# Row sums of softmax weights: a product with a column of ones in place of transposes and a reduction

## The chip, the cores and the metric

The kernel runs on one core of one Trainium2 chip. Five engines work side by side, each through its own queue in order: TensorE (PE; its weight loads are listed as PEld), VectorE (DVE), ScalarE (ACT), GpSimd (POOL), and SyncE (SP), which issues all DMAs here. Matmul results land in PSUM (eight banks of 128 partitions by 512 float32), all else is in SBUF or in device memory. The metric is the device time of one execution in microseconds (us).

## What is computed

One layer of a streaming encoder, float32, 2048 rows of width 1024. The input is projected once (`u = x @ w_in`), and its columns feed three groups: forgetting attention (6 heads of 64, causal), an mLSTM (4 heads of 96) and cross-attention into 256 memory tokens (4 heads of 64). Each group's output is gated, all are concatenated, projected by `w_out`, added to `alpha * x` and normalised. The change touches the softmax of the two attentions:

```python
logits = einsum('bhqd,bhkd->bhqk', q_blk, kh) + c_blk[..., :, None] - c[..., None, :]
p = softmax(where(causal, logits, -inf), axis=-1)     # forgetting attention
out = einsum('bhqk,bhkd->bhqd', p, vh)
...
p = softmax(einsum('bhsd,bhmd->bhsm', qh, kh), axis=-1)   # memory attention
out = einsum('bhsm,bhmd->bhsd', p, vh)
y = concatenate([y_fox * silu(fz), y_ml * silu(mz), y_mem * silu(rz)]) @ w_out
return layer_norm(alpha * x + y)
```

## The kernel before

**Order.** The kernel is written as many small generators (threads). A planner (`Machine`, L135 to L268) runs them once, ahead of time: each thread yields the next instruction or the next buffer that it wants, the planner keeps a clock for every engine, adds an estimated cost to each instruction (`Op.cost`, L91 to L113), and always issues what can start first, ties going to a fixed priority (`PRIO`). The order in which it issues is the order of each engine's queue on the chip. So a changed cost or a removed instruction can shift the order on all engines. All instructions are issued from one line, L214, so the profile's groups are told apart by their tiles.

**Precision.** Large products run in a reduced float32 format in three passes on split operands (`h` and `l`: a high part and the rest). Plain float32 matmuls stand only in the mLSTM, on four heads of 96.

**Stages.** The first 1040 us or so are projections (tiles `pj<-h,h`, `pj<-l,h`, `pj<-h,l`) with the attention between them: each (head, block of 512 queries) is an item, 24 of the forgetting and 16 of the memory attention. Then follow the mLSTM units and the output tiles (`pj<-h,yh` and so on) with their layer norm.

**An item.** `att_max` computes scores of queries by keys (`mx<-km,qm`) for row maxima, which go through a small transpose (`mx<-ident_r,r`) and a DMA into an extra row of the query tile. `att_qk` computes the scores again with keys on partitions and queries along columns (`st<-qm,km`, `st<-qb,kb`, four chunks of 128 keys per block). `att_exp` makes from each chunk the weights twice on ACT (`ph` rounded, `p` exact) and the low part `pl` on DVE; `acc`, the sum over chunks of `p`, is kept by POOL. It has 128 partitions by 512 queries, and what is still missing of a softmax denominator is the sum over its 128 partitions. `att_pv` multiplies by the values into a bank `o`.

**The end of an item** (`att_end`, L702) takes `o` to SBUF and then forms the denominators. Four transposes on PE turn the four 128x128 pieces of `acc` into a bank `mx` (`mx<-ident_r,acc`), and one DVE reduction along columns leaves 128x4 sums in `den` (`den<-mx`). Two heads share a `den` of 128x8. When both are there, `pair_end` (L729) takes the reciprocal, splits it in two parts (`r`), transposes them (`mx<-ident_r,r`, 16x128), moves them by four small DMAs into `rb`, spreads them over partitions by a matmul with `sel`, and scales `y`. Then the gate and the store into `yt_scr` follow. The PSUM tag `mx` has two banks, which `att_max`, `att_end` and `pair_end` share.

Of the kernel before, what the change touches and what calls it, by code (L numbers as in the profile page):

```python
# [12 lines left out]
F32 = mybir.dt.float32  # L13
# [3 lines left out]
ALU = mybir.AluOpType  # L17
AX = mybir.AxisListType
# [3 lines left out]
P = 128  # L22
# [51 lines left out]
class Op:  # L74


    def __init__(self, eng, fn, args, kw):
        self.eng, self.fn, self.args, self.kw = eng, fn, args, kw
        ap = [a for a in args if hasattr(a, "tensor")]
        out = kw.get("out", ap[0] if ap else None)  # L80
        ins = ap[1:] if "out" not in kw else ap
        ins = ins + [v for k, v in kw.items() if k != "out" and hasattr(v, "tensor")]
        self.out = out.tensor.name
        self.ins = [a.tensor.name for a in ins]
        size = lambda a: math.prod(a.shape[1:])
        cols = size(out)
        wide = max([cols] + [size(a) for a in ins])

        there = [a for a in ins if a.tensor.space == "SB" and size(a) > 1]
        self.port = len(there) > 1 if eng in ("DVE", "POOL") else False  # L90
        if eng == "PE":  # L91
            f32 = ins[0].dtype == F32
            if f32 and fn.__name__ != "transpose":
                self.cost = 2.0 * max(2.0 * cols / 2.4, 112.0)
            else:
                self.cost = max((2.0 if f32 else 1.0) * cols / 2.4 + 14.0, 110.0)
        elif eng == "ACT":
            self.cost = 70.0 + 0.835 * wide + 115.0 * sum(hasattr(kw.get(a), "tensor") for a in ("bias", "scale"))
        elif fn.__name__ == "tensor_tensor_scan":
            self.cost = 60.0 + 2.3 * wide  # L100
        elif eng == "DVE":
            one = fn.__name__ in ("tensor_scalar", "tensor_copy")
            columns = sum(size(a) == 1 for a in ins)
            self.cost = 69.0 + (0.521 if one else 1.042) * wide + 60.0 * columns
        elif eng == "POOL":
            if kw.get("op") == ALU.pow:
                self.cost = 290.0 + 170.0 * cols
            else:
                self.cost = 120.0 + (2.15 if fn.__name__ == "tensor_tensor" else 0.95) * wide
        else:  # L110
            self.cost = 475.0
            self.nbytes = 4 * math.prod(out.shape)
            self.far = 800.0 if kw["in_"].tensor.space == "DRAM" else 0.0  # L113
# [21 lines left out]
class Machine:  # L135
# [22 lines left out]
    def free(self, *tiles):  # L158
        for t in tiles:
            nm = t.tensor.name  # L160
            tag, obj = self.tag_of.pop(nm)
            self.seq += 1
            time = max(self.wr.get(nm, (0.0, ""))[0], self.rd.get(nm, 0.0))
            heapq.heappush(self.slots[tag], (time, self.seq, obj))
# [51 lines left out]
    def spawn(self, gen, prio):  # L216
        self.seq += 1
        self.step(Thread(gen, prio, self.seq), None)
# [99 lines left out]
def kernel(ctx: ExitStack, tc: tile.TileContext, xt, x, wg, memt, wm, wo, cw, gb, ng, lg, lb, out):  # L318
# [20 lines left out]
    for tag_, n_ in BUFS.items():  # L339
        m.tag(tag_, n_)  # L340
    PE, ACT, DVE, POOL, SP = (Engine(a, b) for a, b in (("PE", nc.tensor), ("ACT", nc.scalar), ("DVE", nc.vector),
                                                         ("POOL", nc.gpsimd), ("SP", nc.sync)))
    mm = PE.matmul
    now = m.issue

    def const(shape, dt, name):
        return cp.tile(shape, dt, tag=name, name=name)
# [4 lines left out]
    def dma(out, in_):  # L352
        fix = lambda a: a.bitcast(F32) if a.dtype == F32R else a
        return SP.dma_start(out=fix(out), in_=fix(in_))
# [11 lines left out]
    ident = ident_r.bitcast(F32)  # L366
# [9 lines left out]
                           base=0, channel_multiplier=-1))  # L376
    ones_c = const([FH, 1], F32, "ones_c")
    now(POOL.memset(ones_c, 1.0))
    mhalf = const([P, LH], F32, "mhalf")
    now(POOL.memset(mhalf, -0.5))  # L380
    gb_sb = const([P, 14], F32, "gb_sb")
# [295 lines left out]
    def att_pv(it):  # L677

        yield lambda: turn["pv"] == it["i"]
        o = yield Alloc("o")  # L680
        held, nch = None, len(it["chunks"])
        for ci, (km, kb, j, i, q0, dg) in enumerate(it["chunks"]):
            nq = BLK - q0
            last = ci == nch - 1
            yield lambda: ci in it["w"]
            ph, pl = it["w"].pop(ci)
            v_ = it["v"](i, j)
            yield mm(o[:, q0:BLK], v_, ph[:, 0:nq], start=(ci == 0), stop=False)
            free(ph)
            if it["hold"] and ci == 0:  # L690
                held = (v_, pl)
            else:
                yield mm(o[:, q0:BLK], v_, pl[:, 0:nq], start=False, stop=last and not it["hold"])
                free(pl)
            if last and it["hold"]:
                yield mm(o, *held, start=False, stop=True)
                free(held[1])
        turn["pv"] += 1
        it["pv_done"]()
        spawn(att_end(it, o), PRIO["fin"])  # L700

    def att_end(it, o):  # L702


        hh, key = it["hh"], it["ykey"]
        hs, other = slice(64 * hh, 64 * hh + 64), slice(64 - 64 * hh, 128 - 64 * hh)
        if hh == 0:
            ybox[key] = yield [Alloc("y", [P, BLK]), Alloc("sm", [P, 8], F32, "den")]
        yield lambda: key in ybox
        y, den = ybox[key]  # L710
        yield ACT.copy(y[hs, :], o[other, :])
        yield DVE.tensor_tensor(y[hs, :], o[hs, :], y[hs, :], op=ALU.add)
        free(o)
        yield lambda: it["added"] == len(it["chunks"]) - 1
        acc = it["acc"]
        t_ = yield Alloc("mx")
        for s in range(4):
            yield PE.transpose(t_[:, s * P:(s + 1) * P], acc[:, s * P:(s + 1) * P], ident)
        free(acc)
        yield DVE.tensor_reduce(den[:, 4 * hh:4 * hh + 4], t_.rearrange("p (s k) -> p s k", s=4), axis=AX.X,  # L720
                                op=ALU.add)
        free(t_)
        yleft[key] = yleft.get(key, 2) - 1
        if not yleft[key]:
            spawn(pair_end(it, y, den), PRIO["fin"])
# [3 lines left out]
    def pair_end(it, y, den):  # L729


        r_ = yield Alloc("sm", [P, 2, 2, 4], F32R, "r16")
        d2 = den.rearrange("p (h s) -> p h s", h=2)
        yield [DVE.reciprocal(den, den),
               DVE.tensor_copy(r_[:, :, 0, :], d2),
               DVE.tensor_tensor(r_[:, :, 1, :], d2, r_[:, :, 0, :].bitcast(F32), op=ALU.subtract)]
        free(den)
        t_ = yield Alloc("mx")
        yield PE.transpose(t_.bitcast(F32R)[0:16, 0:P], r_.rearrange("p a b c -> p (a b c)"), ident_r)
        free(r_)  # L740
        rr = yield Alloc("rr", [16, P], F32R)
        yield DVE.tensor_copy(rr, t_[0:16, 0:P])
        free(t_)
        rb = yield Alloc("rb")
        for h in range(2):
            for i in range(2):
                yield dma(out=rb[32 * h + i:32 * h + i + 1, :], in_=rr[8 * h + 4 * i:8 * h + 4 * i + 4, :])
        free(rr)
        t_ = yield Alloc("mx")
        yield mm(t_, sel[0:66, :], rb[0:66, :], start=True, stop=True)  # L750
        free(rb)
        yield DVE.scalar_tensor_tensor(y, y, 0.5, t_, op0=ALU.mult, op1=ALU.mult)
        free(t_)
        yield lambda: it["zk"] in zbox
        z_ = zbox.pop(it["zk"])
        b, k = it["dst"]
        yield POOL.tensor_tensor(y, y, z_, op=ALU.mult)
        free(z_)
        h_, l_ = yield [Alloc(YTAGS, [P, BLK], F32R, "yh"), Alloc(YTAGS, [P, BLK], F32R, "yl")]
        yield ACT.copy(h_, y)  # L760
        yield POOL.tensor_tensor(l_, y, h_.bitcast(F32), op=ALU.subtract)
        free(y)
        for i, t_ in enumerate((h_, l_)):
            yield dma(out=yt_scr[b][i][:, k, :], in_=t_)
            free(t_)
        yparts[b] += 1
        if sum(yparts) == 5 * NBLK:
            late.extend(("acc", "ph", "pl", "y", "qb", "p"))
# [109 lines left out]
    cols = {}  # L878
# [583 lines left out]
```

## Time and profile before

| | before |
|---|---|
| Time, median of 3 runs (lowest to highest) | 1351.32 us (1348.97 to 1353.2) |
| Time of the profiled execution | 1350.54 us |
| Its span | 1348.8 us |
| Mean granted clock of TensorE | 0.989 |
| Transposes `mx<-ident_r,acc` on PE | 160, from 84.6 to 1121.3 us |
| Reductions `den<-mx` on DVE | 40, from 87.5 to 1122.4 us |

The profile is one execution. Groups are printed as line, engine, operation, out<-in with tile names (a number behind a name is left out), partitions and shapes, count, then busy us, mean ns of one, and the engine's idle time just before them with what ended it. Timeline rows are start (us), duration (us), engine, operation, tiles and count; a bracket at the end holds the idle time before the row and who ended it. The duration of a PE row contains its way through the array, and the next one starts before it ends, so PE's pace is read from starts.

### The profile page before, as it was taken

How to read it: one execution, taken by the hardware profiler on the slowest of the kernel's cores; microseconds unless marked ns; L12 is line 12 of the kernel's file. 1: busy time of each engine (PE TensorE's matmuls, PEld its weight loads, DVE VectorE, ACT ScalarE, POOL GpSimd, SP SyncE). 2: the span in 40 equal slices, each digit the busy share in tenths (PEclk: the TensorE clock that was granted, in tenths of full speed). 3: DMA queues.
4: the chain of work that ended last, by engine and by line, in shares of the span. 5: the costliest groups of instructions: out<-in, count | busy, mean ns of one | idle time of the engine just before them, and what ended most of it. 6: DMA issues, size and time to landing. Idle time of an engine off the chain costs nothing. (4 is left out here: it accounts for less than half of the span.)

```text
span 1348.8 us, 20536 instructions
## 1 busy us (share of the span) xinstructions
PE 1303.4 (97%) x6648; PEld 1102.1 (82%) x6648; DVE 1011.3 (75%) x2042; ACT 639.6 (47%) x1347; POOL 483.3 (36%) x430
## 2 busy tenths in 40 slices
PE   7999999999999999999999999999999889899997
PEld 7889987877888878988878978887778567788886
DVE  6694457888886578668777787879889788576764
ACT  6343254645654454423545546354463666455400
POOL 3002021334351101310644737263461676455210
PEclk9999999999999999999999999999999799999999
DMA  7624356742336672271421341335227648999761
GB/s 273 200 63 137 125 162 218 242 146 88 122 132 228 229 220 78 96 227 64 138 54 38 109 128 38 106 122 169 87 77 252 194 127 234 274 246 286 227 210 48
DMA packets 176731, 209.50 MB, mean 155 GB/s; under 512 B 15936, under 2 KB 113488, under 8 KB 176624
## 3 DMA queue, kind: packets, MB, share of 16 engines
q1 hardware_dynamic: 176624, 208.19, 49.2%
q8 instruction: 53, 0.87, 0.3%
q14 instruction: 54, 0.44, 0.1%
HBM read 124.88 MB, written 74.41 MB: 148 GB/s over the span
## 5 line engine op out<-in xcount | busy, mean ns | idle before, releaser
L214 POOL TENSOR_TENSOR acc<-acc,p 128x512 f32<-128x512 f32 (+2 forms) x232 | 315.6, 1360 | 434.8 <-ACT p L214 189.3
L214 PE MATMUL pj<-h,h 128*128 128x512 f32 (+3 forms) x1144 | 425.4, 372 | 11.7 <-ACT h L214 9.8
L214 PE MATMUL pj<-l,h 128*128 128x512 f32 (+3 forms) x1144 | 419.3, 367 | 0.6 <-DVE l L214 0.4
L214 PE MATMUL pj<-h,l 128*128 128x512 f32 (+3 forms) x1144 | 418.4, 366 | 0.0
L214 PEld LDWEIGHTS pj<-h,h 128*128 128x128 f32 x1144 | 217.0, 190 | 41.0 <-ACT h L214 11.2
L214 PEld LDWEIGHTS pj<-l,h 128*128 128x128 f32 x1144 | 216.9, 190 | 28.7 <-DVE l L214 2.7
L214 PEld LDWEIGHTS pj<-h,l 128*128 128x128 f32 x1144 | 215.9, 189 | 25.5 <-DVE l L214 0.6
L214 DVE TENSOR_TENSOR pl<-p,ph 128x512 fp32r<-128x512 f32 (+2 forms) x191 | 183.9, 965 | 34.1 <-ACT p L214 29.4
L214 ACT ACTIVATE ph<-st 128x512 fp32r<-128x512 f32 (+2 forms) x224 | 122.8, 555 | 99.4 <-PE st L214 89.5
L214 DVE TENSOR_TENSOR l<-raw,h 128x512 fp32r<-128x512 f32 (+2 forms) x170 | 111.9, 678 | 40.1 <-ACT h L214 38.5
L214 ACT ACTIVATE p<-st 128x512 f32<-128x512 f32 (+2 forms) x232 | 125.5, 546 | 32.2 <-POOL acc L214 16.8
L214 ACT CAST h<-raw 128x512 fp32r<-128x512 f32 (+2 forms) x170 | 96.3, 580 | 70.9 <-DMA raw<-in_wg_dram 48.5
L214 DVE TENSOR_REDUCE mp<-mx 128x1 f32<-128x512 f32 x144 | 95.9, 683 | 22.6 <-PE mx L214 21.8
L214 PE MATMUL st<-qm,km 68*128 68x512 f32 (+2 forms) x272 | 104.5, 384 | 7.7 <-ACT p L214 4.5
L214 PE MATMUL st<-qb,kb 128*128 128x512 f32 (+2 forms) x272 | 110.1, 405 | 0.0
L214 PE MATMUL pj<-h,yh 128*128 128x512 f32 (+1 forms) x264 | 106.9, 405 | 3.2 <-DVE yl L214 2.2
L214 PE MATMUL o<-pl,v 128*128 128x512 f32 (+2 forms) x272 | 104.1, 387 | 6.2 <-DVE pl L214 5.8
L214 PE MATMUL pj<-l,yh 128*128 128x512 f32 (+1 forms) x264 | 102.2, 387 | 0.0
L214 PE MATMUL pj<-h,ylo 128*128 128x512 f32 (+1 forms) x264 | 102.0, 386 | 0.0
L214 PE MATMUL mx<-km,qm 66*128 66x512 f32 (+2 forms) x304 | 97.0, 357 | 2.8 <-issue 1.2
L214 PE MATMUL o<-ph,v 128*128 128x512 f32 (+2 forms) x224 | 84.7, 379 | 0.0
L214 POOL TENSOR_TENSOR y<-y,zs 128x512 f32<-128x512 f32 x20 | 29.5, 1477 | 140.0 <-DVE y L214 80.3
(183 smaller groups left out, 1902.4 us busy)
## 6 DMA issues: line engine op xcount, KB each, us to landing
raw<-in_wg_dram SPq DMA_DIRECT2D x52, 256.0 KB
raw<-in_wg_dram SPq DMA_DIRECT2D x48, 192.0 KB
v<-v_all SPq DMA_DIRECT2D x36, 256.0 KB
raw<-in_xt_dram SPq DMA_DIRECT2D x32, 256.0 KB
yh<-yt_scr SPq DMA_DIRECT2D x32, 256.0 KB
ylo<-yt_scr SPq DMA_DIRECT2D x32, 256.0 KB
xr<-in_x_dram SPq DMA_DIRECT2D x32, 256.0 KB
out_dram<-xr SPq DMA_DIRECT2D x32, 256.0 KB
```

Of the source, the lines that this page charges most:

```text
L214: op.fn(*op.args, **op.kw)
```

## The change

A constant tile `ones_p`, 128x1, is filled with ones. In `att_end` the four transposes of `acc` become four matmuls with the piece of `acc` as weights and `ones_p` as the moving side: each gives a 128x1 column, the sum over partitions, so that four columns of an `mx` bank hold what the reduction gave. The reduction on DVE goes; in its place stands the reciprocal of these 128x4 sums, straight from PSUM into `den`, and the reciprocal of 128x8 in `pair_end` goes. The planner's cost of a plain float32 matmul is lowered for one column, from 2 x 112 to 2 x 64 ns.

```diff
             if f32 and fn.__name__ != "transpose":
-                self.cost = 2.0 * max(2.0 * cols / 2.4, 112.0)
+                self.cost = 2.0 * max(2.0 * cols / 2.4, 112.0 if cols > 1 else 64.0)
...
+    ones_p = const([P, 1], F32, "ones_p")
+    now(POOL.memset(ones_p, 1.0))
...
         for s in range(4):
-            yield PE.transpose(t_[:, s * P:(s + 1) * P], acc[:, s * P:(s + 1) * P], ident)
+            yield mm(t_[:, s:s + 1], acc[:, s * P:(s + 1) * P], ones_p, start=True, stop=True)
         free(acc)
-        yield DVE.tensor_reduce(den[:, 4 * hh:4 * hh + 4], t_.rearrange("p (s k) -> p s k", s=4), axis=AX.X,
-                                op=ALU.add)
+        yield DVE.reciprocal(den[:, 4 * hh:4 * hh + 4], t_[:, 0:4])
...
-        yield [DVE.reciprocal(den, den),
-               DVE.tensor_copy(r_[:, :, 0, :], d2),
+        yield [DVE.tensor_copy(r_[:, :, 0, :], d2),
```

On PE, in the projections of the second half of the sequence, the burst of the first item there keeps its place. Before:

```order
L214 MATMUL pj_7586<-l_5511,h_6980 128x512
L214 MATMUL pj_7586<-h_5510,l_6981 128x512
L214 MATMUL mx_7619<-ident_r,acc_7297 128x128 x4
L214 MATMUL pj_7586<-h_5513,h_6980 128x512
L214 MATMUL pj_7586<-l_5514,h_6980 128x512
L214 MATMUL pj_7586<-h_5513,l_6981 128x512
```

The same place on PE with the change:

```order
L214 MATMUL pj_7574<-l_5503,h_6968 128x512
L214 MATMUL pj_7574<-h_5502,l_6969 128x512
L214 MATMUL mx_7607<-ones_p,acc_7285 128x1 x4
L214 MATMUL pj_7574<-h_5505,h_6968 128x512
L214 MATMUL pj_7574<-l_5506,h_6968 128x512
L214 MATMUL pj_7574<-h_5505,l_6969 128x512
```

Only the four instructions differ; their neighbours are the same matmuls (names are numbered anew). On DVE, the last pair of the first half, before:

```order
L214 TENSOR_REDUCE den_6579<-mx_6592 128x4
L214 TENSOR_TENSOR pl_6604<-p_6600,ph_6599 128x512
L214 TENSOR_TENSOR g_1387_6104<-pj_6555,gb_sb 128x14
L214 TENSOR_TENSOR pl_6609<-acc_6598,ph_6539 128x512
L214 TENSOR_TENSOR vs_6621<-pj_6555,vs_6621 128x6x64
L214 TENSOR_TENSOR y_6578<-o_6593,y_6578 64x512
L214 TENSOR_REDUCE den_6579<-mx_6649 128x4
L214 RECIPROCAL den_6579<-den_6579 128x8
L214 CAST r_1513_6660<-den_6579 128x2x4
```

The same pair on DVE with the change:

```order
L214 RECIPROCAL den_6537<-mx_6560 128x4
L214 TENSOR_TENSOR vs_6566<-pj_6519,vs_6566 128x6x64
L214 TENSOR_TENSOR pl_6582<-acc_6569,ph_6488 128x512
L214 TENSOR_TENSOR pl_6591<-p_6571,ph_6570 128x512
L214 TENSOR_TENSOR y_6536<-o_6561,y_6536 64x512
L214 SCALAR_TENSOR_TENSOR y_6392<-y_6392,mx_6593 128x512
L214 RECIPROCAL den_6537<-mx_6614 128x4
L214 CAST r_1512_6625<-den_6537 128x2x4
```

Each reduction became a reciprocal, the reciprocal of 128x8 is gone, and the scaling of the pair before (`y<-y,mx`) now stands between the two heads. On PE where the projections end, before (`pj<-h,l` at the fourth row is the last projection matmul; `mx<-km,qm` are scores for the maxima of the last item, `st` scores of the item ahead of it):

```order
L214 MATMUL mx_11612<-km_104,qm_108 128x512
L214 MATMUL pj_11509<-h_5718,h_10644 128x512
L214 MATMUL pj_11509<-l_5719,h_10644 128x512
L214 MATMUL pj_11509<-h_5718,l_10645 128x512
L214 MATMUL mx_11623<-km_103,qm_108 128x512
L214 MATMUL st_11615<-qm_110,km_102 128x512
L214 MATMUL st_11615<-qb_10953,kb_10980 128x512
L214 MATMUL mx_11658<-km_103,qm_108 128x512
L214 MATMUL st_11664<-qm_110,km_102 128x512
L214 MATMUL st_11664<-qb_10953,kb_10980 128x512
L214 MATMUL mx_11668<-km_103,qm_108 128x512
L214 MATMUL pj_11684<-mq_11510,mk_11511 128x128 x4
```

There with the change (the last projection matmul is the tenth row):

```order
L214 MATMUL mx_11651<-km_107,qm_110 128x512
L214 MATMUL st_11641<-qm_112,km_104 128x512
L214 MATMUL st_11641<-qb_10950,kb_10980 128x512
L214 MATMUL o_11561<-pl_11635,v_10408 128x512
L214 MATMUL pj_11506<-h_5702,h_10634 128x512
L214 MATMUL pj_11506<-l_5703,h_10634 128x512
L214 MATMUL pj_11506<-h_5702,l_10635 128x512
L214 MATMUL pj_11506<-h_5710,h_10634 128x512
L214 MATMUL pj_11506<-l_5711,h_10634 128x512
L214 MATMUL pj_11506<-h_5710,l_10635 128x512
L214 MATMUL st_11669<-qm_112,km_106 128x512
L214 MATMUL st_11669<-qb_10950,kb_11001 128x512
```

The last of the `mx<-km,qm` now stands six projection matmuls ahead of the end, and none follows; before, eight more of these scores came after the last projection. Behind the last projection matmul stand 64 score matmuls `st` before and 56 with the change.

## The prediction

> **What bounds the kernel now.** First the shares and the slices of the page, then the program cut into three stretches, then the stretches in which the sums stand.
>
> ```profile
> PE 1303.4 (97%) x6648; PEld 1102.1 (82%) x6648; DVE 1011.3 (75%) x2042; ACT 639.6 (47%) x1347; POOL 483.3 (36%) x430
> ...
> PE   7999999999999999999999999999999889899997
> ...
> DVE  6694457888886578668777787879889788576764
> ...
> 84.00:1122.00 1038.00, 1015.12 (x5057) 853.25 (x5056) 801.51 (x1504) 513.02 (x1032) 382.55 (x303) 0.99 0.43 138
> ...
> 800.00:1040.00 240.00, 236.18 (x1137) 194.80 (x1136) 208.54 (x328) 121.78 (x235) 115.66 (x82) 1.00 0.36 117
> 1040.00:1100.00 60.00, 48.48 (x220) 33.89 (x219) 47.79 (x108) 37.73 (x94) 35.69 (x29) 0.86 0.57 167
> ...
> 1040.00:1064.00 24.00, 17.30 (x54) 10.75 (x53) 19.58 (x45) 12.44 (x29) 9.49 (x8) 0.73 0.74 227
> ```
>
> A window row holds the stretch, its length, the busy us of PE, PEld, DVE, ACT and POOL with their instructions, the granted clock, and the DMA share and rate. The sums of the softmax weights run from 84 to 1122 us, and there PE is busy for 1015 of 1038 us. A busy PE is not proof of a full PE, but the timelines below show its matmuls starting one right after the other, at 0.23 us for 512 columns. So in this stretch **PE sets the pace**, and a microsecond of PE work added there is a microsecond on the end, unless it falls on a place where PE waits. Such a place of any size is one only: 1040 to 1064 us, where the projections run out. There PE idles 6.7 of 24 us and has a clock of 0.73, which is worth another 0.27 x 24 = 6.5 us. DVE is busy for 75% over all, and for 80 to 87% from 800 to 1100 us: near, but not the bound. What counts in the change is therefore first what it does to PE.
>
> **PE: transposes out, sums in.** Forty items (24 of the forgetting attention, 16 of the memory attention) each lose four transposes and get four matmuls with one moving column. The row of transposes, and what the stream does around one burst of them:
>
> ```profile
> L214 PE MATMUL mx<-ident_r,acc 128*128 128x128 f32 x160 | 24.6, 272 | 0.0
> ...
> 84.38 0.34 PE L214 MATMUL pj<-h,l 128*128 128x384 f32 x1
> 84.56 0.60 PE L214 MATMUL mx<-ident_r,acc 128*128 128x128 f32 x4
> 84.91 0.42 PE L214 MATMUL pj<-h,h 128*128 128x384 f32 x1
> 85.17 0.34 PE L214 MATMUL pj<-l,h 128*128 128x384 f32 x1
> 85.35 0.33 PE L214 MATMUL pj<-h,l 128*128 128x384 f32 x1
> ```
>
> I count a burst from its first start to the start of the second matmul behind it, less one ordinary step, because the first matmul behind a burst is stretched (0.42 against 0.34). That is 85.17 - 84.56 - 0.18 = **0.43 us for four transposes**.
>
> The new matmuls are plain float32 with 128 weight columns (the sums are the weights, the ones the moving side). Such matmuls exist in the mLSTM, four to a call:
>
> ```profile
> 1181.80 1.03 PE L214 MATMUL pj<-vv,dd 128*128 128x97 f32 x8
> 1182.61 0.47 PE L214 MATMUL pj<-h,yh 128*128 128x512 f32 x1
> 1182.92 0.39 PE L214 MATMUL pj<-l,yh 128*128 128x512 f32 x1
> 1183.15 0.40 PE L214 MATMUL pj<-h,ylo 128*128 128x512 f32 x1
> ...
> 1197.79 1.06 PE L214 MATMUL pj<-mq,mk 96*128 96x128 f32 x8
> 1198.60 0.48 PE L214 MATMUL pj<-h,yh 128*128 128x512 f32 x1
> 1198.91 0.39 PE L214 MATMUL pj<-l,yh 128*128 128x512 f32 x1
> ...
> 1207.75 0.84 PE L214 MATMUL pj<-vw,kr 128*96 128x97 f32 x8
> 1208.37 0.48 PE L214 MATMUL pj<-h,yh 128*128 128x512 f32 x1
> 1208.69 0.39 PE L214 MATMUL pj<-l,yh 128*128 128x512 f32 x1
> ```
>
> Four calls are x8 in the trace: a float32 matmul is two instructions, each with a weight load of its own. By the same count the first burst (97 moving columns, 128 weight columns) takes 1182.92 - 1181.80 - 0.23 = 0.89 us, the second (128 moving) 1198.91 - 1197.79 - 0.23 = 0.89 us, the third (97 moving, 96 weight columns) 1208.69 - 1207.75 - 0.23 = 0.71 us. Fewer moving columns change nothing; fewer weight columns make it shorter. So **the weight loads set the pace, 0.89 / 8 = 0.111 us for 128 columns**, and a stream cut to one column leaves it standing. The load rows say the same, and a lone short stream too:
>
> ```profile
> L214 PEld LDWEIGHTS mx<-ident_r,acc 128*128 128x128 f32 x160 | 19.7, 140 | 3.4 <-issue 0.2
> ...
> L214 PEld LDWEIGHTS pj<-vv,dd 128*128 128x128 f32 x128 | 16.4, 191 | 2.1 <-ACT kr L214 1.1
> ...
> L214 PEld LDWEIGHTS pj<-vw,kr 128*96 128x96 f32 x128 | 12.8, 164 | 0.7
> ...
> 207.95 0.22 PE L214 MATMUL mx<-ident_r,r 128*8 128x128 f32 x1
> 208.01 0.45 PE L214 MATMUL pj<-h,h 128*128 128x512 f32 x1
> 208.29 0.39 PE L214 MATMUL pj<-l,h 128*128 128x512 f32 x1
> 208.53 0.40 PE L214 MATMUL pj<-h,l 128*128 128x512 f32 x1
> ```
>
> The load in plain float32 takes 191 ns against 140 for the same tile in a transpose. The small transpose at 207.95 streams for 0.06 us, yet costs the stream 208.29 - 207.95 - 0.23 = 0.11 us, since the 128-column load of the matmul behind it cannot hide under so short a stream. Every one of the eight new instructions stands in that position. I take **0.89 us for a burst**: 0.89 - 0.43 = +0.46 us, times 40 items = **+18.4 us of PE**. The bounds: no less than 40 x (8 x 0.06 - 0.43) = +2 us, if each cost only the 0.06 us of that short stream; no more than 40 x (8 x 0.191 - 0.43) = +44 us, if the loads followed each other without overlap. The value is close to rows with the same load, so the ends are far less likely than the middle.
>
> The Trainium skill (TensorE: Matmul & The Clock Gate, LDWEIGHTS) speaks against the change in the same way: a load takes the number of weight columns divided by 1.2 ns, whatever the rows. By it an instruction would cost 107 ns and the change an estimated 40 x (8 x 0.107 - 0.43) = +17 us; the trace, at 111, agrees.
>
> **DVE: a reduction out, smaller reciprocals in.**
>
> ```profile
> L214 DVE TENSOR_REDUCE den<-mx 128x4 f32<-128x512 f32 x40 | 27.5, 687 | 8.6 <-PE mx L214 8.0
> ...
> L214 DVE RECIPROCAL den<-den 128x8 f32<-128x8 f32 x20 | 3.9, 196 | 0.2
> ...
> L214 DVE RECIPROCAL sc<-sc 128x4 f32<-128x4 f32 x16 | 2.8, 178 | 0.6
> ...
> PEld o L214 <- DVE pl L214: 15.2, 26, 1.4
> PE o L214 <- DVE pl L214: 5.8, 10, 1.0
> ```
>
> Gone are 40 x 687 ns and 20 x 196 ns = 31.4 us; new are 40 reciprocals of 128x4, which I price by the like one in the mLSTM, 178 ns: 7.1 us. DVE loses **24.3 us of 1011**. Little of it reaches the end: PE waited 5.8 us for DVE's low parts (pl) in front of its matmuls, and the 15.2 us of the loads lie mostly under running matmuls. Bounds 0 and -15, the whole of the load row; I take **-2 us**, since the den reductions are 40 of 2042 instructions in that queue. The latency from the summed tile to its reciprocal stays about equal: +0.46 us on PE, -0.5 on DVE. An mx bank is not held longer. The new memset of ones_p is one POOL instruction at the start, ahead of work of POOL that nobody waits for yet: nothing, and under 1 us if not hidden.
>
> **What the planner moves.** It now prices a burst at 4 x 128 = 512 ns and drops the reduction, so the order of every engine shifts. In most bursts the place is the same. Where the projections end it is not: before, nine score matmuls for the last item's maxima stand among and behind the last projection matmuls; now they are all ahead, and 56 instead of 64 score matmuls are left for the attention alone. That is the stretch 1040 to 1064 us:
>
> ```profile
> 1055.50 0.71 DVE L214 BATCH_NORM_STATS2 sc<-so 128x6 f32<-128x96 f32 x4
> ...
> 1057.89 0.60 ACT L214 ACTIVATE ta<-st 128x512 fp32r<-128x512 f32 x1 [3.81 <-DMA qk_scr<-cv]
> ...
> 1059.03 0.79 PE L214 MATMUL st<-qm,km 68*128 68x512 f32 x1 [3.27 <-ACT p L214]
> ```
>
> PE waits 3.27 us for an exponential that itself waited 3.81 us for the store of a convolution tile, because it had been given that tile's buffer. With another order such a meeting may go, or come at another place. The stretch holds 6.7 + 6.5 = 13.2 us to be had; at worst the new order loses a few us elsewhere, say 3. I take **-5 us**.
>
> **The sum** against the profiled execution, whose time is 1350.54 us (1.7 us around a span of 1348.8; the median of the runs is 0.8 higher): 1350.5 + 18.4 - 2 - 5 = **1362 us**.
>
> **Rivals.**
> 1. *The loads are hidden or quicker than in the mLSTM* (the other side: faster). If a one-column matmul's load ran as the transposes' does, 191 - 140 = 51 ns less, an instruction would cost 111 - 51 = 60 ns, the short stream's 0.06 again. Then the burst is 0.48 us, PE gains 2 us of work, and with the same -7 the time is 1345.5. It decides below 8p - 0.43 = 0.07, p = 63 ns: under that the kernel is faster by over 0.3%, 4 us, which is about what a measurement of it can tell from no change. For it: the planner's new price in the diff is 64, and its other PE prices for such shapes, 110 and 2 x 112, fit the rows (0.43 / 4 and 0.89 / 4). Against it: 97 and 128 columns at the same 0.89. Chance 0.12. The same page of the Trainium skill (Wait — 56ns, not 53.3ns?) says that starts come no closer than about 25 ns however short the stream; if streams alone set the pace, an estimate by it would be 8 x 25 = 200 ns a burst and -9 us. No row here shows such a step behind a 128-column load.
> 2. *The loads cost what I say, but the end of the projections gives nearly all back*: -13 there and -4 from DVE, 1350.5 + 18.4 - 17 = 1352. For it: the order there changed most. Against: it needs every wait of 24 us gone. Chance 0.08.
> 3. *More than the loads*: the bursts are almost without streaming, and the granted clock falls where PE works little (0.73 above); or loads that short streams do not overlap at all. From 0.56 us a burst more, +22 us: 1374 and above. Against: the lone short stream costs 0.11, not more, and a burst is under a microsecond. Chance 0.08.
>
> My forecast has 0.72; its own range is 1355 to 1373. To leave out no more than 2 in 10, the range takes in rival 2 and goes down to 1349. Faster: most of rival 1, 0.10. Same: the rest of it, most of rival 2 and the lower edge of the forecast, 0.11. Slower: 0.79.
>
> **What would show it.** In the changed profile: 320 matmuls mx<-ones_p,acc with a load of some 190 ns each, and bursts that take 0.89 us by the count above (right), or 0.5 (rival 1). DVE's busy time near 987 us. The stretch where the projections end with less PE idle and a clock nearer to 1 (term of -5), or as before. Wrong would be a burst under 0.6 us, a clock that falls at bursts, or new waits of PE of over 5 us in all.

## The result, and the profile after

| | before | with the change |
|---|---|---|
| Time, median | 1350.14 us | 1374.1 us (1371.58 to 1375.5) |
| Ratio | | **1.0175** (95% interval 1.0158 to 1.0191) |
| Span of the profiled execution | 1348.8 us | 1372.5 us |

The change is slower by 24 us. The forecast had the sign and 12 us, half of the size; the time is at the top end of its range (1373 us). The shares on the page of the changed kernel, and one window row of it (stretch, length, busy us of PE, PEld, DVE, ACT, POOL, granted clock, DMA):

```profile
PE 1324.1 (96%) x6808; PEld 1124.9 (82%) x6808; DVE 985.8 (72%) x2022; ACT 640.3 (47%) x1347; POOL 484.5 (35%) x431
...
0.00:1040.00 1040.00, 1016.87 (x5163) 871.60 (x5164) 759.78 (x1433) 494.97 (x957) 346.53 (x305) 1.00 0.42 135
```

PE has 160 instructions more and 20.7 us more busy time, DVE 25.5 us less (the forecast said 987). The clock is 1.00 over these 1040 us, which hold 37 of the 40 bursts: rival 3's falling clock is not there. The new groups, by form, and a burst in the order of time on PE:

```profile
L214 PEld LDWEIGHTS mx<-ones_p,acc 128*128 128x128 f32 x320 | 41.7, 191 | 1.8
L214 PE MATMUL mx<-ones_p,acc 128*128 128x1 f32 x320 | 38.3, 239 | 0.0
...
L214 DVE RECIPROCAL den<-mx 128x4 f32<-128x4 f32 x40 | 7.2, 179 | 16.2 <-PE mx L214 16.0
...
84.47 0.34 PE L214 MATMUL pj<-h,l 128*128 128x384 f32 x1
84.66 0.95 PE L214 MATMUL mx<-ones_p,acc 128*128 128x1 f32 x8
85.46 0.42 PE L214 MATMUL pj<-h,h 128*128 128x384 f32 x1
85.72 0.33 PE L214 MATMUL pj<-l,h 128*128 128x384 f32 x1
85.90 0.33 PE L214 MATMUL pj<-h,l 128*128 128x384 f32 x1
```

There are 320 loads of 191 ns, and a burst counted as in the prediction takes 85.72 - 84.66 - 0.18 = 0.88 us; over the bursts that stand whole between projection matmuls the starts give a median of 0.896 against 0.441 before. Rival 1, loads that run quicker, is out on this alone, and so is the planner's price of 2 x 64 ns. The bursts add 40 x 0.455 = 18 us. The result is 24: where do 6 more come from, and where are the 7 that were to be gained?

### The profile page after: what moved, and what is told of

The parts are those of the page before. It is cut to its first block, busy times and chain, and to the rows that moved or that the text cites. A ratio compares the mean times of both kernels' runs of the same rounds, so it can differ in the third digit from the quotient of the medians.

```text
span 1372.5 us, 20822 instructions
## 1 busy us (share of the span) xinstructions
PE 1324.1 (96%) x6808; PEld 1124.9 (82%) x6808; DVE 985.8 (72%) x2022; ACT 640.3 (47%) x1347; POOL 484.5 (35%) x431
## 4 chain that ended last, share of the span: by engine, by line
PE 77%; DVE 9%; DMA 7%; ACT 2%; issue 2%; SPq 1%; POOL 1%; DVEq 0%; ACTq 0%; POOLq 0%
PE pj L214 56%; PE st L214 7%; PE o L214 7%; PE mx L214 6%; DVE pl L214 2%; DMA dd<-m_scr 1%; SPq L214 1%; DVE cv L214 1%; DVE mp L214 1%; DMA raw<-in_wg_dram 1%; DVE l L214 1%; DVE mx L214 1%; DMA yt_scr<-yl 1%; DMA l<-wo_l 0%; DMA yh<-yt_scr 0%
## 5 line engine op out<-in xcount | busy, mean ns | idle before, releaser
L214 POOL TENSOR_TENSOR acc<-acc,p 128x512 f32<-128x512 f32 (+2 forms) x232 | 318.6, 1373 | 455.0 <-ACT p L214 212.0
L214 DVE TENSOR_TENSOR pl<-p,ph 128x512 fp32r<-128x512 f32 (+2 forms) x199 | 200.9, 1015 | 35.1 <-ACT p L214 30.1
L214 ACT ACTIVATE ph<-st 128x512 fp32r<-128x512 f32 (+2 forms) x231 | 126.4, 554 | 104.6 <-PE st L214 87.8
L214 ACT ACTIVATE p<-st 128x512 f32<-128x512 f32 (+2 forms) x232 | 125.6, 544 | 25.5 <-POOL acc L214 13.1
```

The costliest lines, as they stand in the source:

```text
L214: op.fn(*op.args, **op.kw)
```

## Experiments

**Parts and order taken apart.** The planner reads only `Op.cost`. So an instruction can be exchanged and given the cost of the one whose place it takes, and every queue keeps the order of before; or the old instructions can be given the new ones' costs, and stand in the new order. `priced(op, c)` sets a cost. The main edits to the changed kernel (same_order, dve_only, half_cols) and to the kernel before (order_only); the reciprocal of 128x8 in `pair_end` and the memset of `ones_p` are priced by the same rule in each, which is not shown:

```diff
 same_order
-            yield mm(t_[:, s:s + 1], acc[:, s * P:(s + 1) * P], ones_p, ...)
+            yield priced(mm(t_[:, s:s + 1], acc[:, s * P:(s + 1) * P], ones_p, ...), 2.0 * P / 2.4 + 14.0)
-        yield DVE.reciprocal(den[:, 4 * hh:4 * hh + 4], t_[:, 0:4])
+        yield priced(DVE.reciprocal(den[:, 4 * hh:4 * hh + 4], t_[:, 0:4]), 69.0 + 1.042 * BLK)
 order_only
-            yield PE.transpose(t_[:, s * P:(s + 1) * P], ...)
+            yield priced(PE.transpose(t_[:, s * P:(s + 1) * P], ...), 128.0)
-        yield DVE.tensor_reduce(den[:, 4 * hh:4 * hh + 4], ...)
+        yield priced(DVE.tensor_reduce(den[:, 4 * hh:4 * hh + 4], ...), 69.0 + 1.042 * 4)
 dve_only (on same_order)
-            yield priced(mm(t_[:, s:s + 1], acc[...], ones_p, ...), ...)
+            yield PE.transpose(t_[:, s * P:(s + 1) * P], acc[...], ident)
-        yield priced(DVE.reciprocal(den[...], t_[:, 0:4]), 69.0 + 1.042 * BLK)
+        yield priced(DVE.tensor_scalar(den[...], t_[:, 0:4], 1.0, None, op0=ALU.add), 69.0 + 1.042 * BLK)
 half_cols (on same_order)
-            yield priced(mm(t_[:, s:s + 1], acc[:, s * P:(s + 1) * P], ones_p, ...), ...)
+            yield priced(mm(t_[0:64, s:s + 1], acc[:, s * P:s * P + 64], ones_p, ...), ...)
...
```

same_order, expected:

> All instructions of the change, in the order of before (the planner is given the old costs, so only the replaced instructions differ in every queue). Theory A (the bursts cost PE 0.46 us more each, and what the change cost beyond that, some 5 us, is the shifted order): PE work +18.5, DVE relief 0 to -2, so 1367 to 1369 us where before is 1350, ratio 1.0125 to 1.014; bursts of 0.90 us. Rival B (the rest too comes from the new instructions themselves, as waits that the longer bursts cause): 1373 to 1375, ratio 1.017.

Measured: 1359.37 us, ratio **1.0075** (1.0062 to 1.0088), bursts of 0.896 us. In the trace the queues of PE, VectorE, ScalarE and GpSimd have the order of before. The time is less than either theory: PE's 18 us appear as 10.

order_only, expected:

> The instructions of before (transposes, reductions, reciprocals of 128x8), in the order of the changed kernel. Theory A: the shifted order alone costs what same_order lacks, +4 to +6 us, 1354 to 1356, ratio 1.003 to 1.0045. Rival B: the order is worth nothing, 1349 to 1351, ratio within 0.001 of 1.

Measured: 1372.0 us, ratio **1.0169** (1.0154 to 1.0184). Apart from one memset no instruction of before is changed, and the kernel is 22 us slower. Rival B falls, and A's size with it. This figure is not the price of the order in the changed kernel, though: here the planner counts 73 ns for reductions that take 687, so its plan for DVE is false as well. That price is the ratio of the changed kernel to same_order, the same instructions in two orders: 1.0175 / 1.0075 = 1.010, **13 us** (by the ends of the two intervals, 9 to 17).

dve_only, expected:

> Order of before, transposes kept; each reduction of 128x512 is replaced by a VectorE operation on 128x4, and the reciprocals of 128x8 are left out (the sum over columns and the reciprocal are left out of the computation). DVE busy falls by some 24 us. The forecast's term: -2 us, 1348, ratio 0.9985. Theory A: 0 to -1, since PE hardly waits for VectorE where the reductions stand. If the relief were worth -5 or more (below 1345, ratio 0.996), it would have been eaten by something else in the changed kernel.

Measured: 1343.78 us, ratio **0.9957** (0.9942 to 0.9972), by a kernel that leaves out the sums over columns and the reciprocals. This relief of VectorE is worth 5.8 us (4 to 8 by the interval), three times what the forecast took. Its busy time falls from 1011 to 983 us, as the page says:

```profile
PE 1299.8 (97%) x6648; PEld 1100.5 (82%) x6648; DVE 983.4 (73%) x2022; ACT 637.8 (48%) x1347; POOL 482.9 (36%) x431
```

half_cols, expected:

> As same_order, but each new matmul takes only the first 64 of the 128 weight columns (the sums of the other 64 queries of each piece are left out, and take the first half's; one more small reciprocal per item). If the weight load sets the pace by its columns (128 at 0.112, 96 at 0.084 us in the mLSTM): 0.057 us an instruction, burst about 0.5 us, time 16 us below same_order, 1351 to 1353, ratio 1.001 to 1.002. If an instruction costs a fixed 0.11 us whatever its columns: burst 0.90 and the time of same_order, 1367 to 1369.

Measured: 1355.85 us, ratio 1.0048 (1.0032 to 1.0064): between the two. The group by form, a burst, and the weight loads of the same burst:

```profile
L219 PEld LDWEIGHTS mx<-ones_p,acc 128*64 128x64 f32 x320 | 21.9, 137 | 12.4 <-issue 11.6 <-POOL yl L219 0.4 <-DVE y L219 0.2
...
84.15 0.63 PE L219 MATMUL mx<-ones_p,acc 128*64 128x1 f32 x8
84.71 0.45 PE L219 MATMUL pj<-h,h 128*128 128x384 f32 x1
84.99 0.34 PE L219 MATMUL pj<-l,h 128*128 128x384 f32 x1
...
84.15 0.54 PEld L219 LDWEIGHTS mx<-ones_p,acc 128*64 128x64 f32 x8 [0.26 <-issue]
84.71 0.19 PEld L219 LDWEIGHTS pj<-h,h 128*128 128x128 f32 x1
84.82 0.19 PEld L219 LDWEIGHTS pj<-l,h 128*128 128x128 f32 x1
```

The loads got shorter with their columns (191 to 137 ns) and the burst did too, 84.99 - 84.15 - 0.18 = 0.66 us, so the load does set the pace. But 0.66 / 8 = 0.083 us is not the pace inside the burst. The eight loads take 0.54 us from the first start to the last end, and the last of them takes 0.137, so seven steps take 0.40 us, 0.058 each: the 0.057 of the first theory. By their starts in the traces, a new matmul follows the one before it by 0.058 us here and by 0.112 in the changed kernel. The rest of the 0.66 us lies at the two ends of the burst. There the load of the first 64 columns and the next one of 128 start together with their own matmuls (84.15 and 84.71), and the queue of loads idles 12.4 us in front of the new loads, 0.3 us a burst, where with 128 columns it idled 1.8 us in all. Why a load is not started ahead at these two places was not traced. The time is only 3.5 us below same_order, although the bursts are 40 x 0.24 = 9 us shorter; VectorE has 40 reciprocals more here.

**Do the parts add up?** pe_only is same_order with VectorE's load put back:

```diff
         yield [priced(DVE.reciprocal(den[:, 4 * hh:4 * hh + 4], t_[:, 0:4]), 69.0 + 1.042 * BLK),
+               priced(DVE.tensor_reduce(junk, mrow[:, 0:448].rearrange("p (s k) -> p s k", s=4), ...), 0.0)]
```

> As same_order (order of before, the new matmuls), but VectorE keeps its load: each 128x4 reciprocal is followed by a reduction of 128x448 of a constant, so that VectorE spends per item what it spent before. If the parts add up, this is same_order (+0.75%) less the relief of dve_only (-0.43%): +1.1 to +1.25% of before, 1364 to 1367 us, that is PE's +18 us less some 2 us that fall on waits PE had anyway. Rival (the relief is worth nothing once PE is longer, and the waits alone swallow the difference): the time of same_order, 1358 to 1361, +0.75%.

Measured: 1364.9 us, ratio **1.0115** (1.0096 to 1.0134). VectorE is busy for 1005 us here, for 976 in same_order. The parts add up: 1.15% for PE, -0.43% for VectorE, 0.72% together, and 0.75% was measured with both. Of PE's 18 us, 15.5 reach the end, by the interval 13 to 18.

**Is the new order bad because of the false price, or by chance?** Four kernels differ from one of the two in planner costs alone:

```diff
 price112 (on the changed kernel)
-                self.cost = 2.0 * max(2.0 * cols / 2.4, 112.0 if cols > 1 else 64.0)
+                self.cost = 2.0 * max(2.0 * cols / 2.4, 112.0)
 price_both (on price112)
-        yield DVE.reciprocal(den[:, 4 * hh:4 * hh + 4], t_[:, 0:4])
+        yield priced(DVE.reciprocal(den[:, 4 * hh:4 * hh + 4], t_[:, 0:4]), 180.0)
 jit_pe (on the kernel before)
-            yield PE.transpose(t_[:, s * P:(s + 1) * P], ...)
+            yield priced(PE.transpose(t_[:, s * P:(s + 1) * P], ...), 109.0)
 jit_dve (on the kernel before)
-        yield DVE.tensor_reduce(den[:, 4 * hh:4 * hh + 4], ...)
+        yield priced(DVE.tensor_reduce(den[:, 4 * hh:4 * hh + 4], ...), 640.0)
```

price112, expected:

> The changed kernel, with the planner's cost of a one-column float32 matmul put back to 2 x 112 ns, which is what its bursts take. Theory D (the order got worse because the planner was told 64): near same_order, 1358 to 1363 us, ratio 1.006 to 1.010. Theory C (any change of a cost deals out a new order, and the order of before was a good one among many): not distinguished by the price, anywhere from 1358 to 1380, as likely as not above 1366.

price_both, expected:

> As price112, and the cost of the 128x4 reciprocal raised from 73 to the measured 180 ns. Theory D: 1358 to 1363 us, at least as good as price112. Theory C: another order, 1358 to 1380, without relation to price112.

jit_pe, expected:

> The kernel before, with the planner's cost of a transpose of the summed tile at 109 in place of 121 ns (measured: 108 to 109): the same instructions in another order. Theory D: a price nearer to the chip's costs nothing, 1347 to 1352 us. Theory C: slower by 3 to 20 us, 1353 to 1370.

jit_dve, expected:

> The kernel before, with the planner's cost of the reduction of 128x512 at 640 in place of 602 ns (measured: 687): the same instructions in another order. Theory D: 1347 to 1352 us. Theory C: slower by 3 to 20 us, 1353 to 1370.

All measured orders, by the instructions they hold:

| instructions | order from | median us | ratio (95% interval) |
|---|---|---|---|
| old | costs of before | 1349 to 1350 | 1 |
| old | transpose at 109 (jit_pe) | 1356.11 | 1.0048 (1.0033 to 1.0063) |
| old | reduction at 640 (jit_dve) | 1355.06 | 1.0032 (1.0016 to 1.0047) |
| old | costs of the change (order_only) | 1372.0 | 1.0169 (1.0154 to 1.0184) |
| new | costs of before (same_order) | 1359.37 | 1.0075 (1.0062 to 1.0088) |
| new | matmul at 2 x 112 (price112) | 1364.82 | 1.0107 (1.0082 to 1.0132) |
| new | matmul at 2 x 64 (the change) | 1374.1 | 1.0175 (1.0158 to 1.0191) |
| new | 2 x 112, reciprocal at 180 (price_both) | 1380.08 | 1.0219 (1.0194 to 1.0243) |

With the true matmul price the new instructions run 9 us faster than with 64, which speaks for D; with the reciprocal's true price added they run 15 us slower again, which D excludes. And two prices moved nearer to the chip's made the old instructions slower by 4 to 7 us. Theory D falls: the order follows from the costs, but its time is not better where the costs are truer. The table has six orders, since same_order stands in the order of before and order_only in that of the change. For the same work the spread is 1.7% over four orders of the old instructions and 1.4% over four of the new.

**Two other ways to the same sums.** act_sum keeps transposes and order and makes the sum on ScalarE; the planner is still told that this is one reduction on VectorE, so it keeps no time free on ScalarE. bcast swaps the sides of the matmul; what it takes out of `pair_end` is not shown:

```diff
 act_sum (on the kernel before)
-        yield DVE.tensor_reduce(den[:, 4 * hh:4 * hh + 4], ...)
+        sums = [ACT.activation(t_[:, s * P:(s + 1) * P], t_[:, s * P:(s + 1) * P], AF.Identity,
+                               accum_out=den[:, 4 * hh + s:4 * hh + s + 1]) for s in range(4)]
...
 bcast (on the changed kernel)
-            yield mm(t_[:, s:s + 1], acc[:, s * P:(s + 1) * P], ones_p, start=True, stop=True)
+        yield mm(t_, twos, acc, start=True, stop=True)
-        yield DVE.reciprocal(den[:, 4 * hh:4 * hh + 4], t_[:, 0:4])
+        yield [DVE.reciprocal(t_[hs, :], t_[hs, :]),
+               DVE.tensor_tensor(y[hs, :], y[hs, :], t_[hs, :], op=ALU.mult)]
...
```

> Instructions and order of before, with the transposes, but the sum over columns is made on ScalarE: four Identity activations of 128x128 per item with their sum as second output, issued where VectorE's reduction stood. VectorE loses 27 us, ScalarE (busy 47%) gains about 40 x 4 x 0.25 = 40 us. If relief of VectorE is what counts, most of dve_only's -0.43% stays: 1343 to 1348 us, ratio 0.996 to 0.999. If ScalarE's exponentials are as near to the bound: 1350 to 1358.

Measured: 1376.75 us, ratio 1.0206 (1.0186 to 1.0227), worse than both guesses. The groups of act_sum, and its longest wait of PE's loads for ScalarE beside the same wait before:

```profile
L214 ACT ACTIVATE mx<-mx 128x128 f32<-128x128 f32 x160 | 42.6, 266 | 11.9 <-PE mx L214 8.1
L214 ACT ACTIVATION_READ_ACCUMULATOR mx<-mx 128x1 f32 x160 | 31.2, 195 | 0.0
...
PEld st L214 <- ACT acc L214: 14.6, 12, 3.7
```

```profile
PEld st L214 <- ACT acc L214: 2.3, 3, 1.1
```

A sum on ScalarE is two instructions, of 266 and 195 ns, that overlap in part: the engine's busy time rises from 640 to 694 us, by 54 where 40 were assumed. And it stands in the queue of the exponentials: the scores' loads, which need a bank that an exponential frees, wait 14.6 us where they waited 2.3. That is part of the 27 us; the rest was not traced. In this order, a busy share of 47% did not mean room there.

> The ones as weights and the summed tile as the moving side: one reduced-float32 matmul of 512 columns per item gives the sum already spread over all partitions (the last additions on GpSimd write that format, so the sums are rounded once more), and a reciprocal and a product of 64x512 on VectorE replace everything in pair_end up to the gate: its transposes, small DMAs and the matmul with sel. PE per pair of heads: 2 x 0.24 in place of 2 x 0.44 + 0.11 + 0.24, so 15 us less in all; VectorE about as before (2.76 for 2.86 us a pair). The planner deals out a new order, which has cost 5 to 30 us in the runs so far. If PE's work decides: 1335 to 1350. If the order decides: 1350 to 1365.

Measured: 1462.93 us, ratio 1.0838 (1.0819 to 1.0857). One row stands out, the reciprocals of bcast:

```profile
L214 DVE RECIPROCAL mx<-mx 64x512 f32<-64x512 f32 x40 | 134.6, 3365 | 2.4 <-PE mx L214 1.5
...
PEld o L214 <- DVE pl L214: 52.6, 39, 3.9
```

It was priced as any other 512-column operation, 0.69 us, and takes 3.37. These take 107 us more than the reductions did, DVE's busy time rises from 1011 to 1129 us, and the waits of PE's loads for the low parts rise from 15.2 to 52.6 us. This is the likely cause, but no run shows it apart from the new order. So bcast says nothing on its PE side. No complete version that beats the kernel before was found.

## Why the prediction came out as it did

**PE: right.** 0.89 us for a burst, +18.4 us in the sum; measured 0.896 and 18. pe_only shows 15.5 us of time for it (13 to 18), so a few us may fall on waits that PE had anyway, which the sum did not take off. That the weight load sets the pace is shown by half_cols, 0.058 us a matmul with 64 columns and 0.112 with 128. The duration of a load row is not its price, though, as the prediction took it to be beside its 191 and 140 ns: the transposes' loads of 140 ns come at the same pace (four rows of 0.272 us in 0.60 us, so one start every 0.109 us). What doubles the burst is eight instructions in place of four, each at the same pace.

**VectorE: right in sign, wrong in size.** The step "I take -2 us, since the den reductions are 40 of 2042 instructions in that queue" failed: dve_only gives -5.8, and same_order against pe_only 1.0075 / 1.0115, -5.3. The bounds (0 to -15) held it. The number was read from PE's waits for DVE alone. One wait that is shorter in the trace of dve_only stands under another engine's name; first a PE row of the kernel before, then the same matmul in dve_only, then in same_order, where VectorE is relieved as well:

```profile
609.10 0.44 PE L214 MATMUL pj<-h,h 128*128 128x384 f32 x1 [1.65 <-ACT h L214]
...
604.00:614.00 10.00, 8.07 (x34) 6.68 (x33) 5.45 (x11) 3.22 (x6) 0.63 (x2) 0.83 0.64 203
```

```profile
603.45 0.44 PE L219 MATMUL pj<-h,h 128*128 128x384 f32 x1 [0.60 <-ACT h L219]
...
599.00:609.00 10.00, 9.11 (x48) 7.72 (x47) 5.53 (x11) 3.36 (x7) 0.63 (x2) 1.00 0.63 194
```

```profile
617.90 0.69 PE L219 MATMUL pj<-h,h 128*128 128x384 f32 x1 [1.88 <-ACT h L219]
...
613.00:623.00 10.00, 7.52 (x29) 6.01 (x28) 5.90 (x12) 3.21 (x6) 0.63 (x2) 0.83 0.62 191
```

PE waits 1.65 us for a weight cast of ScalarE before, and the 10 us around have a clock of 0.83; in dve_only the wait is 0.60 and the clock stays at 1.00, worth another 1.7 us. But each trace is one execution, and in same_order the wait (1.88) and the lower clock (0.83) are there again. So this place is not shown to be a part of the 5.8 us. What both pairs of kernels share is smaller: PE's loads wait for the low parts 15.2 us before and 13.6 in dve_only, and 13.6 in pe_only and 11.7 in same_order. That the relief is worth some 5 us is shown by two pairs of runs; by which waits it reaches the end stays open.

**The order: wrong in sign.** The step "With another order such a meeting may go, or come at another place ... I take -5 us" failed; the order costs 13 us, beyond the 3 that were allowed at worst. The reading of the place was not wrong: the maxima are all ahead of the last projection. (Of the 64 and 56 `st` matmuls behind it, 8 each are the mLSTM's `st<-mcol_b,ident_b`, so 56 and 48 are the attention's; the difference of eight stands.) But it gained nothing. From the last projection to the last sums, and from there to the end, before:

```profile
1041.00:1121.00 80.00, 68.48 (x346) 50.93 (x346) 65.03 (x142) 52.50 (x133) 50.09 (x39) 0.89 0.60 173
1121.00:1349.00 228.00, 213.55 (x1180) 180.12 (x1178) 151.76 (x409) 85.68 (x240) 87.29 (x85) 0.99 0.74 217
```

and with the change:

```profile
1065.00:1132.00 67.00, 57.36 (x273) 43.31 (x272) 53.66 (x106) 42.58 (x104) 46.04 (x36) 0.85 0.48 135
1132.00:1373.00 241.00, 224.90 (x1242) 189.06 (x1242) 148.84 (x430) 90.16 (x259) 87.63 (x86) 0.99 0.75 219
```

PE's idle time and its lost clock in the first stretch are 11.5 + 0.11 x 80 = 20.3 us before and 9.6 + 0.15 x 67 = 19.7 after. The stretch is 13 us shorter, but only because it holds 73 matmuls less: most of them now stand behind it, the others ahead of the last projection. And the order was not changed there alone. The time between starts on PE beyond what each form takes in a dense stream, for the same instructions in the two orders (worked out from the starts in the two traces; how much counts as dense shifts both columns alike, and the difference of the sums is that of the two spans, 15.7 us):

| stretch (cut at the same projection matmuls) | same_order, us | the change, us |
|---|---|---|
| start to the 200th group of projection matmuls | 3.9 | 4.2 |
| to the 500th | 6.2 | 10.9 |
| to the 800th | 10.7 | 9.0 |
| to the 1100th | 11.6 | 16.0 |
| to the last projection | 1.2 | 1.6 |
| to the last sums | 21.4 | 22.9 |
| to the end | 9.3 | 15.4 |
| sum | 64.3 | 80.0 |

The loss has no one place. It is also the sign of being wrong that the prediction named last, new waits of PE of over 5 us in all. In the waits, the largest rise that can be named is that of PE's loads waiting for VectorE's low parts, first same_order, then the change:

```profile
PEld o L219 <- DVE pl L219: 11.7, 20, 1.4
```

```profile
PEld o L214 <- DVE pl L214: 18.1, 26, 1.5
```

The forecast valued a new order at the one place where the old one waited. The old order's waits can be seen in the trace and the new one's cannot, so such a count can come out only as a gain. What bounds the term instead is the spread of orders: the five other orders in the table cost 4 to 23 us, all of them on the slow side, which a forecast made from one trace could not know. The 3 us that the prediction allowed at worst came from no row.

**The sum** was +18.4 - 2 - 5 = 11.4. In its place the runs show +15.5 for PE, -5.4 for VectorE and +13 for the order, 23 us, beside 24 measured. The 13 us are the change measured against same_order, so it is pe_only, not this sum, that tests the parts. The sign came out right by its mechanism, PE's longer bursts. That the time lies no further off is luck: PE and VectorE came out 6 us below their terms and the order 18 us above its own.

**Rivals.** The first is out by the burst. Its price of 60 ns rested on the load rows of 140 and 191 ns, which are not the pace; and the planner's price of one of these transposes is 121 ns (jit_pe), not the 110 that was quoted for it. The second is out by the stretch above (20.3 and 19.7 us). The third is out by the burst and by the clock of 1.00 in the row of 0 to 1040 us; the time is the 1374 us that it named, but not by its way, and its own sum, 1350.5 + 22, comes to 1373, or 1366 with the -7.

What stays open is why the order of before is better than the five others tried, and why the true price of the reciprocal made it worst. No single wait was found to which it could be put down.

## What to carry to other kernels

A product with a column of ones is not cheap for its one column: in float32 it costs two loads of the whole tile as weights, and beside a full PE stream that is twice the price of a transpose. Where a planner sets the order, an edit has two prices, that of its instructions and that of the new order; give the new instructions the old costs, so that the order stays, and the two can be measured apart. And a forecast should give a new order a spread, not the removal of the waits that the old trace shows; here all five other orders were on the slow side.

## What the runs showed of the hardware that was not expected

From one start to the next, a pair of float32 load and one-column matmul took 0.112 us with 128 weight columns and 0.058 with 64; the pairs of 96 weight columns in the mLSTM (with 97 moving columns) took 0.085. That is some 0.84 ns a column, and it holds from 128 columns down to 64. But a burst of 64-column loads among loads of 128 cost 0.66 us, 0.083 a pair, because its ends were not hidden. VectorE's reciprocal took 179 ns for 128x4 and 3365 ns for 64x512, some 6.3 ns for each further column, where a reduction of 128x512 took 687 ns in all. A sum as second output on ScalarE is an instruction of its own, 195 ns beside each activation of 266; 160 of both raised its busy time by 54 us. Taking 28 us of busy time off VectorE, which was busy for 75%, gave 5.8 us.
